# A column-group tail of three k tiles instead of four, with the last joined tile moved into the last column group's tail

## Chip, cores, metric

One core of one Trainium2 chip. The metric is device time of the whole kernel in microseconds, median of several executions. A profile is one execution, and its span is about 1.8 us shorter than the time of that execution.

## The reference

```python
B, S, D, W = 4, 4096, 4096, 64       # x [B,S,D], w [D,D] float32, offsets [B]
for b in range(B):
    o = int(offsets[b])
    results.append(x[b, o:o+W] @ w)  # 64 rows of each batch times the whole of w
```

So 256 rows are multiplied by a 4096 x 4096 matrix: 67 MB of w are read once, 4.2 MB are written. The rows are two stationary sets of 128 (`G = 2`); w has 32 k tiles of 128 rows.

## The kernel before

w is loaded by DMAs that cast to fp16 on the way. k tiles 1 to 27 come as blocks of whole rows, in buffers of four tiles, of which there are three. The last tiles (the tail) come as two column groups of 2048, so that the first group (`order[0]`) can be finished and stored while the last group (`order[1]`) still loads. The last two blocks of whole rows are the joined tiles: their products are not summed by themselves, but within the passes of the two column groups.

```python
blocks = [(0, 1), (1, 2), (3, 4), (7, 4), (11, 4), (15, 4), (19, 3), (22, 3), (25, 2), (27, 1)]
n_join = 2
k_tail = 28
...
order = [1, 0]
steps = [(ki, 2, 0, NG) for ki in range(k_tail, n_k, 2)]   # tail loads, per column group
...
join = range(blocks[-n_join][0], k_tail)                   # tiles 25, 26, 27
...
columns(order[1], list(join))               # last group: a first pass over the joined tiles
ng = order[0]
columns(ng, list(join) + list(range(k_tail, n_k)))         # first group: everything
for g in range(G):
    store(nc.gpsimd, g, ng * NG, (ng + 1) * NG)
ng = order[1]
k_fine = n_k - n_fine                       # the last two tiles, finer
for ki in range(k_tail, k_fine):            # last group: its tail
    for g in range(G):
        for j in range(n_sub):
            tail_mm(ki, g, ng, j, ki == k_tail, False)
q = [nc.scalar, nc.sync]
for g in range(G):
    for h in range(2):
        ...                                 # matmuls of tiles 30, 31, then one add
        add_out(4 * g + js[0], 2, g, ng * n_sub + js[0])
    store(q[g], g, ng * NG, (ng + 1) * NG)
```

`columns` runs the matmuls of one group, then adds half of the eight PSUM banks to the accumulator on VectorE, copies the other half out on ScalarE, and adds that too. The loads and the first group's stores are issued by GpSimd in one queue.

## Time and profile before

| | before |
|---|---|
| time, median | 181.62 us (181.52 to 181.75, 6 runs) |
| last load issued / landed | 134.12 / 169.14 us |
| first group's stores issued | 166.19 and 167.32 us |
| last store issued / landed | 174.88 / 179.0 us |

Here is the end of TensorE's timeline (start, duration, instruction, in brackets the idle time before it and what ended it):

```profile
149.24 14.42 PE L185 MATMUL banks<-wc,xT 128*128 128x512 f16 x64 [0.42 <-DMA wc<-in_w_dram]
164.29 3.63 PE L185 MATMUL banks<-wc,xT 128*128 128x512 f16 x16 [0.64 <-DMA wc<-in_w_dram]
169.18 3.61 PE L185 MATMUL banks<-wc,xT 128*128 128x512 f16 x16 [1.26 <-DMA wc<-in_w_dram]
```

TensorE finishes the first group at 163.66 and waits for loads three times: it has time to spare, 1.26 us of it ahead of the last stage. The first group's stores in GpSimd's timeline, and the last store's line among the DMA issues (KB, us from issue to landing):

```profile
166.19 0.55 POOL L231 DMA_DIRECT2D out_dram<-acc  x1 [31.34 <-DVE acc L244]
167.32 0.54 POOL L231 DMA_DIRECT2D out_dram<-acc  x1 [0.58 <-DVE acc L244]
...
out_dram<-acc SPq DMA_DIRECT2D x1, 1024.0 KB, 4.1
```

### The profile page before, as it was taken

Reading aid. Unit: us, or ns where it says so; the run is one execution under the profiler, and the core shown is the slowest. Engines: PE = TensorE matmul, PEld = TensorE weight load, DVE = VectorE, ACT = ScalarE, POOL = GpSimd, SP = SyncE. Lnnn points to the kernel's source line nnn. Section 1 sums busy time; section 2 is a strip of 40 time slices with the busy share of each in tenths; the row PEclk is TensorE's granted clock in tenths of the full one; section 3 lists DMA queues with packets and bytes.
Section 4 is the critical chain, followed back from the end, with each engine's and each line's share of the span. In section 5 each row is a group of like instructions: output and inputs, shape, how many; then the busy total and the mean of one; then the engine's idle time right before and its main releaser. Section 6 shows DMA issues by size and latency. Waiting matters only on the chain.

```text
span 179.9 us, 1393 instructions
## 1 busy us (share of the span) xinstructions
PE 123.0 (68%) x578; PEld 56.3 (31%) x578; DVE 83.2 (46%) x75; ACT 16.8 (9%) x15; POOL 11.1 (6%) x24
## 2 busy tenths in 40 slices
PE   1000007996399919990799649999939998998740
PEld 1000007642144404440344214444414443443310
DVE  2000004844046725662076605669956956308280
ACT  2402102644000000000000000000000004004000
POOL 4400000001000010001000100002060000000200
PEclk9999999999879999999699988999999999999997
DMA  6999997999999899999989999999999999999976
GB/s 200 315 261 215 226 262 168 219 237 233 226 226 211 189 197 233 237 219 226 219 189 197 233 220 208 217 224 202 235 200 219 191 211 216 212 215 214 363 337 288
DMA packets 3399, 40.97 MB, mean 228 GB/s; under 512 B 322, under 2 KB 322, under 8 KB 1346
## 3 DMA queue, kind: packets, MB, share of 16 engines
q0 software_dynamic: 2816, 36.70, 93.2%
q1 hardware_dynamic: 432, 3.15, 4.5%
q10 hardware_dynamic: 146, 1.05, 1.4%
q8 instruction: 4, 0.07, 0.1%
q14 instruction: 1, 0.01, 0.0%
HBM read 71.30 MB, written 4.19 MB: 420 GB/s over the span
## 4 chain that ended last, share of the span: by engine, by line
DMA 66%; PE 24%; POOL 2%; issue 2%; DVE 2%; DVEq 1%; POOLq 0%
DMA wc<-in_w_dram 66%; PE banks L185 24%; POOL wc L149 1%; DVE acc L195 1%; DVEq L292 1%; POOL xrow L131 1%; POOL wc L88 0%; DVE rows L122 0%; PE banks L119 0%; POOL below L100 0%; DVE rows L110 0%; POOL below L99 0%; DVE ones L115 0%; DVE off_f L116 0%; POOLq L100 0%
## 5 line engine op out<-in xcount | busy, mean ns | idle before, releaser
L185 PE MATMUL banks<-wc,xT 128*128 128x512 f16 x496 | 116.2, 390 | 22.5 <-DMA wc<-in_w_dram 22.4
L195 DVE TENSOR_TENSOR acc<-acc,banks 128x1024 f32<-128x1024 f32 x56 | 67.9, 1220 | 58.8 <-PE banks L185 57.6
L185 PEld LDWEIGHTS <-xT 128*128 128x128 f16 x512 | 50.7, 100 | 88.7 <-DMA wc<-in_w_dram 23.6
L171 PE MATMUL banks<-identity,xrow 128*128 128x128 f16 x64 | 5.2, 262 | 24.2 <-DMA xrow<-in_x_dram,rows 24.2
L180 DVE CAST xT<-banks 128x1024 f16<-128x1024 f32 x4 | 4.7, 1221 | 25.0 <-PE banks L171 25.0
L240 ACT COPY tmp<-banks 128x1024 f32<-128x1024 f32 x4 | 3.9, 1016 | 116.2 <-PE banks L185 116.2
L171 PEld LDWEIGHTS <-xrow 128*128 128x128 f16 x64 | 5.1, 127 | 24.3 <-DMA xrow<-in_x_dram,rows 24.3
L88 POOL DMA_DIRECT2D wc<-in_w_dram x9 | 5.0, 566 | 113.5 <-PE banks L185 112.7
L213 DVE COPY acc<-banks 128x1024 f32<-128x1024 f32 x4 | 4.9, 1225 | 4.6 <-PE banks L185 4.6
L185 PE MATMUL banks<-w,xT 128*128 128x512 f16 x16 | 6.1, 379 | 0.0
L182 ACT CAST xT<-banks 128x1024 f16<-128x1024 f32 x4 | 3.9, 1018 | 11.6 <-PE banks L171 11.6
L244 DVE TENSOR_TENSOR acc<-acc,tmp 128x1024 f32<-128x1024 f32 x4 | 4.7, 1218 | 0.0
L215 ACT COPY acc<-banks 128x1024 f32<-128x1024 f32 x4 | 4.0, 1012 | 6.5 <-PE banks L185 6.5
L149 POOL DMA_DIRECT2D wc<-in_w_dram x4 | 2.8, 721 | 9.3 <-PE banks L185 9.3
L231 POOL DMA_DIRECT2D out_dram<-acc x2 | 1.1, 549 | 31.9 <-DVE acc L244 31.9
L74 ACT CAST w<-acc 128x2048 f16<-128x2048 f32 x1 | 1.9, 1897 | 8.9 <-DMA acc<-in_w_dram 8.9
L119 PE MATMUL banks<-off_f,ones 1*128 1x4 f32 x2 | 0.6, 358 | 3.1 <-DVE off_f L116 3.1
L73 ACT CAST w<-acc 128x2048 f16<-128x2048 f32 x1 | 1.9, 1897 | 3.4 <-DMA acc<-in_w_dram 3.4
L110 DVE TENSOR_REDUCE rows<-below 128x1 f32<-128x128 f16 x1 | 0.3, 286 | 2.6 <-POOL below L100 2.6
L119 PEld LDWEIGHTS banks<-off_f,ones 1*128 1x128 f32 x2 | 0.5, 304 | 3.1 <-DVE off_f L116 3.1
L73 ACT ACT_TABLE_LOAD x1 | 1.3, 1283 | 1.3 <-PEq L281 1.3
L131 POOL DMA_INDIRECT xrow<-in_x_dram,rows x1 | 1.0, 1026 | 1.6 <-DVE rows L122 1.6
(11 smaller groups left out, 2.4 us busy)
## 6 DMA issues: line engine op xcount, KB each, us to landing
wc<-in_w_dram POOLq DMA_DIRECT2D x4, 4096.0 KB, 42.2
wc<-in_w_dram POOLq DMA_DIRECT2D x2, 3072.0 KB, 35.7
wc<-in_w_dram POOLq DMA_DIRECT2D x5, 1024.0 KB, 27.0
wc<-in_w_dram POOLq DMA_DIRECT2D x2, 2048.0 KB, 19.8
acc<-in_w_dram SPq DMA_DIRECT2D x2, 1024.0 KB, 10.5
out_dram<-acc POOLq DMA_DIRECT2D x2, 1024.0 KB, 6.1
out_dram<-acc ACTq DMA_DIRECT2D x1, 1024.0 KB, 3.9
out_dram<-acc SPq DMA_DIRECT2D x1, 1024.0 KB, 4.1
```

What stands on the lines that cost most here:

```text
L73: nc.scalar.copy(out=w_one[:, :NG], in_=w0_32[:, :NG])
L88: nc.gpsimd.dma_start(out=t[:, base : base + r * N], in_=w[k0 * P : (k0 + r) * P, :].rearrange("(p r) n -> p (r n)", r=r),)
L149: nc.gpsimd.dma_start(out=t[:, pos : pos + n * wd].rearrange("p (t n) -> p t n", t=n), in_=w[ki * P : (ki + n) * P, ng * NG + c0 : ng * NG ...
L171: nc.tensor.matmul(out=pairs[t][:, i * P : (i + 1) * P], lhsT=x_cols(g, 8 * t + i), rhs=identity[:], start=True, stop=True,)
L180: nc.vector.tensor_copy(out=dst, in_=pairs[t][:])
L182: nc.scalar.copy(out=dst, in_=pairs[t][:])
L185: nc.tensor.matmul(out=banks(bank), lhsT=xT[g][:, kt * P : (kt + 1) * P], rhs=rhs, start=start, stop=stop,)
L195: nc.vector.tensor_add(out=dst, in0=dst, in1=banks(bank, n))
L213: nc.vector.tensor_copy(out=dst, in_=banks(b0, 2))
L215: nc.scalar.copy(out=dst, in_=banks(b0, 2))
L240: nc.scalar.copy(out=tmp[g][:], in_=banks(4 * g + 2, 2))
L244: nc.vector.tensor_add(out=dst, in0=dst, in1=tmp[g][:])
```

## The change

Its intent: one k tile fewer in the half-row tail, one more in the row blocks (19 becomes a block of four), and less work in the last group's first pass, so that the first group's pass starts sooner.

```diff
-    blocks = [(0, 1), (1, 2), (3, 4), (7, 4), (11, 4), (15, 4), (19, 3), (22, 3), (25, 2), (27, 1)]
+    blocks = [(0, 1), (1, 2), (3, 4), (7, 4), (11, 4), (15, 4), (19, 4), (23, 3), (26, 2), (28, 1)]
     n_join = 2
-    k_tail = 28
+    k_tail = 29
...
-    steps = [(ki, 2, 0, NG) for ki in range(k_tail, n_k, 2)]
+    steps = [(k_tail, 1, 0, NG), (k_tail + 1, 2, 0, NG)]
...
-    columns(order[1], list(join))
+    columns(order[1], list(join)[:-1])
...
-    for ki in range(k_tail, k_fine):
+    for ki in range(k_tail - 1, k_fine):
...
-                tail_mm(ki, g, ng, j, ki == k_tail, False)
+                tail_mm(ki, g, ng, j, ki == k_tail - 1, False)
```

## The prediction

> **What bounds the kernel now.** I read the busy digits of the page first, then the chain, the issue-to-landing times of single loads, the TensorE timeline and one-microsecond windows of the last 20 us. The page:
>
> ```profile
> PE   1000007996399919990799649999939998998740
> DMA  6999997999999899999989999999999999999976
> DMA 66%; PE 24%; POOL 2%; issue 2%; DVE 2%; DVEq 1%; POOLq 0%
> wc<-in_w_dram POOLq DMA_DIRECT2D x4, 4096.0 KB, 42.2
> ```
>
> The 16 DMA engines are busy in almost every slice; TensorE has holes. The last line gives what lands per load: a block of 4 k tiles takes 42 us from issue to landing because another block is ahead of it in the queue. The chain of waits in order of time:
>
> ```profile
> 63.36 0.28 issue
> 63.65 41.99 DMA wc<-in_w_dram
> 105.64 0.05 issue
> 105.69 26.05 PE banks L185 x112
> 131.74 0.28 issue
> 132.02 2.10 POOL wc L149 x3
> 134.12 35.02 DMA wc<-in_w_dram
> 169.14 0.04 issue
> 169.18 1.04 PE banks L185 x4
> ```
>
> A load issued at 63.65 lands at 105.64, and the last tail load lands at 169.14. Adding each load's issue and its time to landing gives block (7,4) 67.0, (11,4) 86.3, (15,4) 105.64, (19,3) 120.1 (twice the median of 35.7 less 32.6, added to 81.28), (22,3) 134.6, (25,2) 144.4, (27,1) 149.2 and the four tail pieces 154.4, 159.3, 164.2, 169.14. So a k tile costs 4.84 us in the blocks of four, 4.82 in those of three, 4.8 to 4.9 in the small blocks, and 4.93 to 5.0 in the half-row tail pieces. 2.097 MB read in 4.84 us is 433 GB/s. **The load stream never starves and sets the time to 169 us.** What follows is the end, in windows (stretch; busy PE, PEld, DVE, ACT, POOL; clock; DMA share; GB/s moved):
>
> ```profile
> 166.00:167.00 1.00, 1.00 (x6) 0.49 (x5) 1.00 (x1) 0.00 (x0) 0.55 (x1) 1.00 1.09 221
> 167.00:168.00 1.00, 0.92 (x5) 0.29 (x3) 0.03 (x1) 0.00 (x0) 0.54 (x1) 1.00 1.01 311
> 168.00:169.00 1.00, 0.00 (x0) 0.00 (x0) 0.00 (x0) 0.00 (x0) 0.00 (x0) 1.00 1.00 401
> ...
> 172.00:173.00 1.00, 0.80 (x4) 0.18 (x2) 1.00 (x2) 0.00 (x0) 0.00 (x0) 1.00 0.47 197
> 173.00:174.00 1.00, 0.00 (x0) 0.00 (x0) 1.00 (x2) 0.00 (x0) 0.00 (x0) 1.00 0.68 287
> 174.00:175.00 1.00, 0.00 (x0) 0.00 (x0) 0.85 (x1) 0.00 (x0) 0.00 (x0) 1.00 0.95 401
> ```
>
> Loads count fp16 bytes written (about 217 GB/s); stores count fp32 bytes (400 and more). So the bytes of the loads end near 167.4, though the last one's completion arrives at 169.14, and the stores of the first finished column group run from 167.4 on. The DMA engines then have about 0.85 us of idle (0.53 + 0.32) in 172 to 174, waiting for the last group's stores, issued at 172.63 and 174.88 and landed 3.9 and 4.1 us later.
>
> **What the Trainium skill says.** (1) "DMA: Bandwidth & Descriptors", section "Where 436 GB/s comes from": the ceiling is 435.2 GB/s from the SBUF ports. The trace agrees: 433 read. A faster load stream is not to be had by reordering. (2) Same page, "Issuing engines are not separate DMA queues": transfers from different issuers interleave on the same 16 engines. The trace agrees: three issuers' stores together never move more than 467 GB/s in a microsecond. (3) Same page, "Anatomy of one DMA": a fit for the GpSimd path of 2.0 us plus bytes over 436 GB/s. For 1.05 MB that is 4.4 us; the trace has 3.9 and 4.1 from the other two issuers, so a last store cannot be shortened here. (4) "TensorE: Matmul & The Clock Gate", Part 1: 215.7 ns per warm 512-column matmul, 426.7 ns cold. The trace agrees: outputs of eight matmuls follow each other by 1.725 us (216 ns each); after the wait that ends at 105.69 the first eight take 3.24 us (405 ns) at a granted clock of 0.58.
>
> **The change, part by part.**
> Unchanged: 512 matmuls of the product, 56 adds of 1220 ns out of PSUM (six blocks with 8 adds before and after, plus the column groups), number of loads, bytes of loads and stores.
>
> *Load stream.* One k tile leaves the half-row tail for a row block, saving 4.95 - 4.84 = 0.1 us. Landings after: (19,4) 105.64 + 4 x 4.84 = 125.0; (23,3) + 14.5 = 139.5; (26,2) + 9.8 = 149.3; (28,1) + 4.8 = 154.1; first group's tail 29 at 156.6 and 30-31 at 161.5; last group's 29 at 164.0 and 30-31 at 169.0.
>
> *Issue of the tail loads.* They reuse the buffer of block 19, so they wait for 4 k tiles rather than 3. TensorE ends (15,4) at 121.4 as before, then idles 3.6 us until 125.0 (before it went straight on, as 120.1 lay behind it), then runs 64 matmuls. That took 15.7 us after idles of 4.06 and 4.02 us and 14.2 us after 3.6 us (67.0 to 81.2). So block 19 ends at 139.2 to 140.7 instead of 131.7, and the tail is issued by 144. The queue has work until 154.1: 10 us of margin, **no starvation**.
>
> *TensorE behind the stream.* Block (23,3) with the two-tile first pass of the last group is 64 matmuls, for which 14.16 us were measured on the same mix: 153.5 to 154.9. The first group's pass then has 24 matmuls (26-28) at 216 ns = 5.2, plus the 0.6 us by which the same stage now exceeds 64 x 216 ns (14.42 against 13.8; banks still being emptied): 159.3 to 160.7. Tile 29 adds 8, 1.7 us: 161.0 to 162.4. Tiles 30-31 (landed 161.5) add 16, 3.45 us. **The first group ends at 165.0 to 165.9, against 163.65 before: 1.3 to 2.2 us later**, because less of it can be done ahead: its last piece lands at 161.5 rather than 159.3.
>
> *Last group before the last landing.* Tiles 28-29 are 16 matmuls as before (3.63 us with the bank wait, some 3.75 here): done at 168.8 to 169.65, against 167.9 before. Before, TensorE waited 1.26 us for the last load; now the last stage begins at 169.0 to 169.65 instead of 169.18: -0.15 to +0.5. The stage itself (16 matmuls, four adds, two stores) is the same.
>
> *Stores of the first group.* They were issued 2.53 and 3.66 us after its last matmul (166.19, 167.32), hence now at 167.5 to 168.4 and 168.7 to 169.6. Before, bytes ran about 1.2 us after issue, just when the loads' bytes ended. Now the store bytes begin at 168.7 to 169.6, so the engines are idle for 1.4 to 2.3 us that they used before. Four stores of 1.05 MB at 435 GB/s need 9.64 us: bytes end at 178.3 to 179.2. Before: 167.4 + 9.64 + 0.85 idle = 177.9 (the windows show about 178.2), landed at 179.0. With the same 0.8 us of completion: 179.1 to 180.0. **Sum: +0.1 to +1.0 us, middle near +0.5**; the 0.1 us saved on loads is in it.
>
> **Rivals.**
> *A: nothing is seen.* If the late stores only fill the 0.85 us hole and the last group starts at 169.0, the end is the last landing plus the same 10 us: 181.6. For it: the hole is there, and TensorE had 1.26 us to spare. Against: the stores shift by more than the hole.
> *B: a real gain.* If the shorter tail lets the half-row transfers go (each k tile 0.1 us dearer), or an idle of TensorE was on the path, 181.0 or so. For it: the tail loads are the dearest bytes. Against: only one of 32 k tiles changes, and the rate is at 433 GB/s already.
> *C: TensorE becomes the bound.* Another cold start at 125.0 and again in the tail would push the first group's end to 167 and the last stage to 171: 183.5. For it: the wait before 125.0 is new, 3.6 us, about the length after which the clock was seen low. Against: from 139.5 on TensorE has hardly any wait, and (7,4) after 3.6 us was not slowed much.
> *D: the load queue runs dry* since the tail is issued 7 to 9 us later. For it: the longer reuse chain. Against: 10 us of margin.
>
> **Range and chances.** Before is 181.72 (181.58 to 181.75). My sum gives +0.5 with a spread of +0.1 to +1.0, rival A pulls down, C up: 182.1. I take 181.3 (A with a part of B) to 183.1 (half of C) as 8 in 10. Over 2% would be under 178.1 or over 185.4; the first needs a load stream above the measured rate, the second needs D or a double C. So 0.02, 0.95, 0.03.
>
> **What would show it.** Right: last load landing within 0.3 us of 169.0; TensorE idle before (19,4) of about 3.6 us and the tail issued near 140; first group's stores issued at 167.5 or later; no hole in the DMA share in 172 to 174 but one near 168; last store issued at 174.7 to 175.4 and landing 4 to 5 us later. Wrong: a last landing clearly before 168.8 (loads cheaper than I think) or after 169.6 (dry queue or slower tail); first group's stores as early as before; a cold clock in the tail.

## The result

| | before | after |
|---|---|---|
| time, median of 6 | 181.62 us (181.52 to 181.75) | 182.63 us (182.37 to 183.77) |
| last load landed | 169.14 | 169.1 |
| first group's stores issued | 166.19, 167.32 | 168.13, 169.28 |
| last store issued, landing | 174.88, 4.1 us | 175.05, 4.7 us |

The ratio of after to before is 1.0068, 95% interval 1.0039 to 1.0096: slower, by well under 2%. A ratio is the mean time of one kernel's fast runs over that of the other's in the same rounds, so it is not quite the ratio of the medians. The spread of these six is larger too, 1.4 us against 0.2; but twelve later runs of the kernel before, beside e1 to e4 below, spread by 1.4 us as well (181.57 to 182.99).

The page of the changed kernel, its busy digits and the shares of the chain:

```profile
PE   1000008998499919993899859982999999999920
DMA  6999998999999989999999999998999999999696
DMA 47%; PE 40%; issue 3%; DVE 3%; another core or an unknown queue 2%; POOL 1%; DVEq 1%; POOLq 0%
```

TensorE's share of the chain went from 24% to 40%, and DMA's digits have a 6 in the third slice from the end, where they had a 9. In the chain in order of time one sees where TensorE took over:

```profile
82.96 42.13 DMA wc<-in_w_dram
125.09 0.05 issue
125.14 27.33 PE banks L185 x118
...
155.95 8.38 PE banks L185 x38
...
166.76 3.63 PE banks L185 x16
```

The chain meets no load after 125.09, the landing of block 19. The TensorE and GpSimd timelines say the same:

```profile
125.14 47.82 PE L185 MATMUL banks<-wc,xT 128*128 128x512 f16 x208 [3.96 <-DMA wc<-in_w_dram]
...
168.13 0.57 POOL L231 DMA_DIRECT2D out_dram<-acc  x1 [24.52 <-DVE acc L244]
169.28 0.53 POOL L231 DMA_DIRECT2D out_dram<-acc  x1 [0.57 <-DVE acc L244]
...
out_dram<-acc SPq DMA_DIRECT2D x1, 1024.0 KB, 4.7
```

After a new wait of 3.96 us, 208 matmuls run in one stretch; none waits for a load again. The first group's stores are issued 1.94 and 1.96 us later. The last store lands 0.8 us later than before: its issue came 0.17 us later, and it takes 0.6 us longer to land. The windows of one microsecond (busy PE, PEld, DVE, ACT, POOL; clock; DMA share; GB/s) show what that does to the DMA engines:

```profile
167.00:168.00 1.00, 1.00 (x6) 0.46 (x5) 1.00 (x2) 0.00 (x0) 0.00 (x0) 1.00 0.52 102
168.00:169.00 1.00, 1.00 (x6) 0.48 (x5) 0.97 (x1) 0.00 (x0) 0.57 (x1) 1.00 0.11 20
169.00:170.00 1.00, 1.00 (x7) 0.41 (x6) 0.00 (x0) 0.00 (x0) 0.53 (x1) 1.00 0.89 377
...
173.00:174.00 1.00, 0.00 (x0) 0.00 (x0) 1.00 (x2) 0.00 (x0) 0.00 (x0) 1.00 1.05 442
```

Where 311 and 401 GB/s were moved before, the engines are now idle for 1.37 us (0.48 + 0.89). The hole that the kernel before had in 172 to 174 is gone: once begun, all four stores run without a pause. In windows of a quarter of a microsecond nothing is moved from 168.5 to 169.25, and the last bytes come at 179.0: 4.19 MB in 9.75 us, or 430 GB/s.

### The profile page after: what moved, and what is told of

Same layout as the page of the kernel before. It is cut to its first block, busy times and chain, and to the rows that moved or that the text cites.

```text
span 180.6 us, 1393 instructions
## 1 busy us (share of the span) xinstructions
PE 128.0 (71%) x578; PEld 58.6 (32%) x578; DVE 83.4 (46%) x75; ACT 17.0 (9%) x15; POOL 10.8 (6%) x24
## 3 DMA queue, kind: packets, MB, share of 16 engines
q10 hardware_dynamic: 146, 1.05, 1.4%
HBM read 71.30 MB, written 4.19 MB: 418 GB/s over the span
## 4 chain that ended last, share of the span: by engine, by line
DMA 47%; PE 40%; issue 3%; DVE 3%; another core or an unknown queue 2%; POOL 1%; DVEq 1%; POOLq 0%
DMA wc<-in_w_dram 47%; PE banks L185 40%; DVE acc L195 2%; DVEq L292 1%; POOL xrow L131 1%; POOL wc L88 0%; DVE rows L122 0%; PE banks L119 0%; POOL below L100 0%; DVE rows L110 0%; POOL below L99 0%; DVE ones L115 0%; DVE off_f L116 0%; POOLq L100 0%
## 5 line engine op out<-in xcount | busy, mean ns | idle before, releaser
L185 PE MATMUL banks<-wc,xT 128*128 128x512 f16 x496 | 120.1, 400 | 17.7 <-DMA wc<-in_w_dram 17.4
L185 PEld LDWEIGHTS <-xT 128*128 128x128 f16 x512 | 51.8, 102 | 86.6 <-DMA wc<-in_w_dram 19.9
L171 PE MATMUL banks<-identity,xrow 128*128 128x128 f16 x64 | 6.5, 299 | 24.1 <-DMA xrow<-in_x_dram,rows 24.1
L171 PEld LDWEIGHTS <-xrow 128*128 128x128 f16 x64 | 6.3, 143 | 24.2 <-DMA xrow<-in_x_dram,rows 24.2
```

The lines of the kernel that those rows point to most:

```text
L171: nc.tensor.matmul(out=pairs[t][:, i * P : (i + 1) * P], lhsT=x_cols(g, 8 * t + i), rhs=identity[:], start=True, stop=True,)
L185: nc.tensor.matmul(out=banks(bank), lhsT=xT[g][:, kt * P : (kt + 1) * P], rhs=rhs, start=start, stop=stop,)
```

## The experiments

Theory T after the result. T1: the late stores of the first group leave the DMA engines idle, and the last store then queues behind them. T2: the clock, low after the new wait, delays TensorE. Rivals: only the start of the last matmul stage counts (R); the block shapes or the smaller tail loads cost time; the first group's stores are hidden anyway. Each run's before is the kernel before on the same chip, in the same rounds; runs of different series are compared by their ratios. There is no e8 on record.

| run | median, us | before, us | ratio (95%) |
|---|---|---|---|
| e1, tail of three alone | 184.03 | 181.72 | 1.0124 (1.011 to 1.0139) |
| e2, moved tile alone | 181.67 | 181.72 | 0.9999 (0.9986 to 1.0012) |
| e3, after, early stores | 182.38 | 181.72 | 1.0036 (1.0023 to 1.0048) |
| e4, after, clock kept up | 182.17 | 181.72 | 1.0028 (1.0015 to 1.0041) |
| e5, before, late stores | 183.25 | 181.63 | 1.0077 (1.0058 to 1.0095) |
| e6, before, half stores | 181.81 | 181.63 | 1.0015 (0.9991 to 1.0039) |
| e7, after, half stores | 182.34 | 181.63 | 1.0048 (1.002 to 1.0077) |
| e9, after, e3 and e4 | 182.07 | 181.63 | 1.0021 (1.0003 to 1.0038) |
| e10, as e9, 15 fillers | 181.92 | 181.76 | 1.0011 (0.9998 to 1.0024) |
| e11, after again | 182.37 | 181.76 | 1.0031 (1.0018 to 1.0044) |
| e12, before, early stores | 181.96 | 181.76 | 1.0007 (0.9993 to 1.0021) |

### The two parts alone

The tail of three without the second part (against the changed kernel):

```diff
-    columns(order[1], list(join)[:-1])
+    columns(order[1], list(join))
-    for ki in range(k_tail - 1, k_fine):
+    for ki in range(k_tail, k_fine):
-                tail_mm(ki, g, ng, j, ki == k_tail - 1, False)
+                tail_mm(ki, g, ng, j, ki == k_tail, False)
```

> The new blocks and the tail of three, but tile 28 stays in the last group's first pass. Theory T (the first group's stores come late, the DMA engines idle before them, and the four stores then run back to back to the end): 8 more matmuls lie ahead of the first group's end, 1.7 us; its stores are issued near 169.9 and 171.0 instead of 168.1 and 169.3, the hole in the DMA share grows by 1.7 us and the time goes from 182.6 to about 184.3. Rival R (only the start of the last matmul stage counts): that stage has 8 matmuls fewer ahead of it in exchange, starts near 169.4 as in the changed kernel, and the time stays at 182.6.

Measured: 184.03. The stores were issued at 169.91 and 171.06, the last stage's first add began at 170.67, only 0.26 us later than in the changed kernel. Windows of this run, and its last store's line:

```profile
168.00:169.00 1.00, 0.89 (x5) 0.32 (x4) 1.00 (x2) 0.49 (x1) 0.00 (x0) 1.00 0.15 29
169.00:170.00 1.00, 1.00 (x6) 0.45 (x5) 1.00 (x2) 0.00 (x0) 0.09 (x1) 1.00 0.00 0
170.00:171.00 1.00, 1.00 (x6) 0.48 (x5) 1.00 (x2) 0.00 (x0) 0.49 (x1) 1.00 0.00 0
...
out_dram<-acc SPq DMA_DIRECT2D x1, 1024.0 KB, 6.2
```

Two whole microseconds pass in which nothing is moved, and the last store lands 6.2 us after its issue, against 4.7. That is T1, and R alone is out: the last stage hardly moved, the time rose by 1.4 (ratios 1.0124 and 1.0068). The second part of the change is thus a repair of the first: it takes 8 matmuls from ahead of the first group's end.

The moved tile alone, on the kernel before (join 25 to 27, tail of four):

```diff
-    columns(order[1], list(join))
+    columns(order[1], list(join)[:-1])
-    for ki in range(k_tail, k_fine):
+    for ki in range(k_tail - 1, k_fine):
-                tail_mm(ki, g, ng, j, ki == k_tail, False)
+                tail_mm(ki, g, ng, j, ki == k_tail - 1, False)
```

> The old blocks and the tail of four, with the last joined tile (27) moved into the last group's tail. T: the first group ends sooner (about 163, set by the landing at 159.3 plus 16 matmuls), its stores are issued by 165.6, but queue behind loads whose bytes end at 167.4: no gain, 181.6 (181.4 to 181.8). The last load is still waited for by TensorE for some 0.7 us. Rival: if a longer tail of the last group costs by itself, 182.2 or more.

Measured: 181.67, the same as before. The stores were issued at 165.21 and 166.34, 1 us sooner than before, and began no sooner: they lie in the queue behind the loads. So the whole loss comes with the tail of three.

### Late stores on the kernel before

```diff
+    nc.gpsimd.tensor_copy(
+        out=x16.bitcast(fp32)[:, :NG], in_=acc[0][:, ng * NG : (ng + 1) * NG]
+    )
     for g in range(G):
         store(nc.gpsimd, g, ng * NG, (ng + 1) * NG)
```

> Kernel before with a GpSimd copy of 2048 columns ahead of the first group's stores, which delays them by d (some 2 us, to be read from the trace) and touches no matmul. T1: up to about 1.2 us the delay fits the idle of the DMA engines between 172 and 174; beyond that every microsecond counts: 181.7 + (d - 1.2), so 182.5 for d = 2, 183.5 for d = 3, with the last store issued at 174.9 as before and landing later. Rival (the first group's stores are hidden anyway): 181.7.

The copy took 2.81 us and the stores were issued from 169.12 on, 2.9 us later than 166.19. The formula gives 181.7 + 2.9 - 1.2 = 183.4; measured 183.25, against 181.63 of its before. GpSimd's timeline, TensorE's last stage and the last store:

```profile
169.12 1.09 POOL L231 DMA_DIRECT2D out_dram<-acc  x2
...
169.22 3.61 PE L185 MATMUL banks<-wc,xT 128*128 128x512 f16 x16 [1.25 <-DMA wc<-in_w_dram]
...
out_dram<-acc SPq DMA_DIRECT2D x1, 1024.0 KB, 5.7
```

The last matmul stage starts as before, with 1.25 us to spare, and the last store was issued at 174.92; it only lands later, 5.7 us after its issue. Late stores of the first group cost time by themselves, with blocks, tail and TensorE unchanged. The rival "hidden anyway" is out.

The traces give T1 as one number. From the issue of the first group's first store to the landing of the last store it is 11.6 us in the changed kernel (168.13 to 179.75), 11.6 in e1 (169.91 to 181.51) and 11.5 here (169.12 to 180.62), and 11.6 to 11.7 in e4, e7 and e11 below: each microsecond of delay is paid in full. In the kernel before it is 12.8 us (166.19 to 178.98), so its stores had 1.2 us to spare. There the end hangs on the last store alone, which lands 4.0 to 4.2 us after its issue in every trace in which the first group's stores were not late (before, e2, e3, e9, e10, e12).

### Clock kept up

12 matmuls whose result is never used, run in the wait before block 19 of the changed kernel:

```diff
     for k0, r in blocks[2:-n_join]:
+        if k0 == 19:
+            for _ in range(12):
+                nc.tensor.matmul(out=banks(0), lhsT=xT[0][:, :P],
+                                 rhs=xT[0][:, :NT], start=True, stop=True)
         whole_rows(range(k0, k0 + r))
```

> Changed kernel with 12 matmuls of no use in the wait before block 19, so that its 64 matmuls start at full clock. T: block 19 ends 1.9 us sooner, but block 23 lands at 139.6 and the first group's last piece at 161.7, so that group ends near 165.2 (0.4 sooner) and the time falls by about 0.4 to 182.2; the spread between runs (182.4 to 183.8) shrinks to some 0.3, as the slow start no longer reaches the end. R (the slow clock is the whole cause): 181.7.

Measured: 182.17, with a spread of 0.3 (182.07 to 182.36), both as T2 said. Block 19's 64 matmuls took 13.97 us, and the last store was issued at 174.80 instead of 175.05. The changed kernel was then run again for a second trace:

> The changed kernel again, for a second trace of it beside these runs: 182.4 to 183.8 by the earlier runs, median 182.6. T2: between 125 and the end its matmuls take another time than the 47.82 us of the first trace if the clock came up sooner or later, and the last store moves with it; the last load lands within 0.2 us of 169.1 all the same.

Median 182.37 (182.11 to 182.50). Against its own before this is 1.0031, and the run with the fillers is 1.0028: the medians do not show that the fillers gain anything, and the spread is only 0.4 without them. TensorE's timeline of this second trace of the same kernel, and its last store:

```profile
124.93 13.99 PE L185 MATMUL banks<-wc,xT 128*128 128x512 f16 x64 [3.61 <-DMA wc<-in_w_dram]
139.43 21.52 PE L185 MATMUL banks<-wc,xT 128*128 128x512 f16 x96 [0.51 <-DMA wc<-in_w_dram]
161.76 10.97 PE L185 MATMUL banks<-wc,xT 128*128 128x512 f16 x48 [0.81 <-DMA wc<-in_w_dram]
...
174.81 0.35 SPq L231 DMA_DIRECT2D out_dram<-acc  x1
...
out_dram<-acc SPq DMA_DIRECT2D x1, 1024.0 KB, 4.7
```

The last store is issued a little before that of the kernel before (174.88), and still lands 0.5 us later: with TensorE undisturbed T1 alone remains.

Here the clock was up by itself after a wait of 3.61 us: block 19 took 13.99 us and was done before block 23 had landed, as in the run with the fillers (182.17 profiled there, 182.19 here). In the first trace the first add after block 19's landing came 3.06 us after the start of its matmuls, against 1.94 us here, and the next 2.29 us later, against 1.73 us; (3.06 - 1.94) + (2.29 - 1.73) = 1.7 us were lost to the low clock. So the changed kernel has two kinds of execution. Of the 1.7 us, 0.24 us reach the last store's issue (175.05 against 174.81). That the slow start makes the spread between runs is not shown (see what stays open, below). In both kinds the first group's stores are late (167.90 and 169.04 even here), since the group's last piece now lands at 161.7 instead of 159.3.

### Early stores, and both remedies

The first group's stores are issued right behind the tail loads with stale data. Its output is wrong, which doesn't matter for the time.

```diff
-    for g in range(G):
-        store(nc.gpsimd, g, ng * NG, (ng + 1) * NG)      # after the first group
...
+    first = order[0]
+    stale = x16.bitcast(fp32)
+    for g in range(G):
+        nc.gpsimd.dma_start(
+            out=out_rows[g, :, first * NG : (first + 1) * NG],
+            in_=stale[:, g * NG : (g + 1) * NG])
     columns(order[1], list(join)[:-1])
```

> Changed kernel, but the first group's stores send stale data (a wrong result on purpose) and are issued right after the tail loads, so they queue straight behind them; TensorE's work is untouched. T: the hole at 167.5 to 169.1 goes, the last store is issued at 175.0 as before the edit of this run and lands in about 4.1 us instead of 4.7: 182.0, 0.6 less than the changed kernel. R (TensorE's lateness) or load shapes: no gain, 182.6.

Measured: 182.38, less of a gain than expected; by the ratios (1.0036, and 1.0031 for the changed kernel again) none. In its trace the last store landed after 4.0 us, not 4.7, so T1's part came out; but TensorE needed 48.83 us for the 208 matmuls instead of 47.82, and issued the last store at 175.90: the granted clock was 0.50 from 125 to 130:

```profile
124.99 48.83 PE L185 MATMUL banks<-wc,xT 128*128 128x512 f16 x208 [3.61 <-DMA wc<-in_w_dram]
...
125.00:128.00 3.00, 3.00 (x8) 1.07 (x9) 0.00 (x0) 0.00 (x0) 0.00 (x0) 0.50 1.11 238
```

In that execution the slow start ate the gain. Its wait, 3.61 us, is the same as in e11, where the clock was up, and in e1 the clock was low after only 2.60 us: in these traces the length of the wait does not tell which start comes. Hence both remedies at once:

> Changed kernel with both remedies: the 12 matmuls that keep the clock up before block 19, and the first group's stores sent early with stale data (a wrong result on purpose). Theory T, now in two parts (T1: the late first-group stores lengthen the last store from 4.1 to 4.7 us; T2: the slow clock after the new wait delays the last matmul stage by 0.2 to 1 us, differently from run to run): last store issued at 174.8, landing 4.0 us later, 181.5, as the kernel before, with a spread under 0.4. If something else in the change costs time (block shapes, the tail's smaller pieces), it stays at 181.9 or more.

The profiled execution was as expected: 181.58, last store issued at 174.85 and landed 4.1 us later. But the median was 182.07, with 182.46 as the highest: a miss by 0.5, and a spread of 0.9 where under 0.4 was expected. Two runs looked for the remainder. The control, early stores in the kernel before:

> Control for the early store: the kernel before, with the first group's stores sent early with stale data (a wrong result on purpose). T1: in the kernel before these stores already begin when the loads' bytes end, so nothing moves: 181.7, last store landing about 4.1 us after its issue. If the early store itself costs time, 182.0 or more, and the 0.4 us that was left over with both remedies is its cost.

Measured 181.96 against 181.76, with the profiled execution at 182.30. Its TensorE line of the last stage:

```profile
169.72 3.61 PE L185 MATMUL banks<-wc,xT 128*128 128x512 f16 x16 [1.72 <-DMA wc<-in_w_dram]
```

The last load's completion came at 169.7 here, though the change from the loads' rate to the stores' took place in 167 to 168 as in the kernel before (283 GB/s in that microsecond, 311 there). To take out small shifts of the whole stream, count from the landing of the first group's last piece to that of the last load. With a tail of four this is 9.8 us in the kernel before, e2, e5 and e6, and 10.3 in e12; with a tail of three it is 7.4 us in the changed kernel, e1, e4, e7 and e11, and 7.6, 7.8 and 7.8 in e3, e9 and e10. So in all four traces with early stores the completion of the load ahead of them came 0.2 to 0.5 us later, and the remedy is not free; why is not shown.

> As the run with both remedies, with 15 matmuls of no use instead of 12, so that the wait before block 19 is nearly filled (3.4 of 3.6 us; a wrong result on purpose again). If the 0.4 us that was left over came from a clock that still dropped in some runs, 181.6 with a spread under 0.4; if from the small margin of TensorE before the last load (0.27 us against 1.26 before) or elsewhere, 182.0 as with 12.

Measured 181.92, spread 0.3. This is the control's 181.96: on one chip and in the same rounds, the changed kernel gave 182.37, with both remedies 181.92, and the kernel before with the same early stores 181.96. With both causes taken away nothing of the change is left to explain, within the noise: the ratios to the kernel before are 1.0011 and 1.0007, each to about 0.0013, so the two differ by 0.1 us, give or take some 0.35. Block shapes and smaller tail loads are bounded by that and no more closely.

### Half stores

The last group's stores are cut in four, each sent after its own add, alternating between ScalarE's and SyncE's queue:

```diff
             add_out(4 * g + js[0], 2, g, ng * n_sub + js[0])
-        store(q[g], g, ng * NG, (ng + 1) * NG)
+            c0 = (ng * n_sub + js[0]) * NT
+            store(q[h], g, c0, c0 + 2 * NT)
```

> Kernel before with the last group's stores cut in four halves, each sent after its own add. T1: the idle of the DMA engines in 172 to 174 is filled and the last store is half as long: bytes end at 167.4 + 9.64 = 177.1 instead of 178.2, time about 180.6. Rival (the last add and a fixed store time set the end): a half store saves 1.2 us, 180.5. The same here; it is the pair with the next run that tells them apart.

> Changed kernel with the last group's stores cut the same way. T1: the DMA engines are busy without a hole from 169.1 to 179.0, so cutting and sending earlier moves nothing: 182.3 to 182.6. Rival (the last add and a fixed store time set the end): 1.2 us less, 181.4.

On the kernel before: 181.81, a miss of 1.2 us. On the changed kernel: 182.34, as expected. The windows of the first and its last store's line:

```profile
173.00:174.00 1.00, 0.00 (x0) 0.00 (x0) 1.00 (x2) 0.00 (x0) 0.00 (x0) 1.00 0.93 381
...
177.00:178.00 1.00, 0.00 (x0) 0.00 (x0) 0.00 (x0) 0.00 (x0) 0.00 (x0) 0.66 0.75 307
```

The hole is filled, as meant, but the last half store still landed 4.1 us after its issue near 174.8, so at 178.9 instead of 179.0. Adding the DMA shares from 167 to 179, the engines were busy for 10.75 us against 10.58 in the kernel before, and in the last microseconds not all of them had work left (0.75, then 0.10). So the hole in 172 to 174 was not worth its 0.85 us: 0.1 us lay in it by the trace, and nothing by the median (181.81 against 181.63). T1's number for this run was wrong, because in the kernel before the end hangs on the last store's issue and landing, not on the bytes of all four stores; and half the bytes did not land sooner. The rival that both kernels gain 1.2 us is out as well. No version beats the kernel before, and none was suggested by the runs: in it the stores begin when the load bytes end, and filling the idle time that is left gained nothing.

## Why the prediction was right, point by point

- **Load stream.** Right. Block 19 landed at 125.09 (125.0 predicted), the last load at 169.1 (169.0). The 0.1 us from the smaller tail cannot be seen: 169.1 against 169.14, and from trace to trace it comes anywhere between 168.8 and 169.2. One reading was not exact: that the loads' bytes end near 167.4. In the changed kernel, where no store covers it, a last part of them runs on, at 115 GB/s and less, until 168.5.
- **Issue of the tail loads.** Right. TensorE idled for 3.96 us (3.6); block 19 was done near 140.8 in one trace and at 138.9 in the other (139.2 to 140.7, so just outside at either end), and no load came late. Rival D is out.
- **First group.** Right, 165.6 (165.0 to 165.9), worked out as the start of its first add, 164.35, plus the 1.26 us by which that add started before the last matmul in the kernel before.
- **Last stage.** Right: it begins 1.06 us before its first add, at 169.35 (169.0 to 169.65).
- **First group's stores.** Right: issued at 168.13 and 169.28, in the stated windows. The hole near 168 and the closed hole near 173 are there. e1 and e5 show that this causes the loss.
- **Bytes end, sum.** Right, term by term. With the measured issue of the first store put in, the sum gives 168.13 + 1.2 + 9.64 + 0.8 = 179.77; the last store landed at 179.75. In the second trace it gives 179.54, and the landing was at 179.51. These are 0.8 and 0.5 us later than before, where +0.1 to +1.0 with a middle of +0.5 was said. The part of the sum that was left wide is when the first group ends, and with it the first store's issue; the low clock moved that from 167.90 to 168.13. I had it as an upper edge of the block's time and as rival C.
- **The medians.** They rose by 1.0 us in the first six runs and by 0.6 in the later five. The first figure is at the very edge of the sum, and more than its own trace shows: two slow executions that were not traced push it up. That it stayed within the sum is in part luck.
- **Rates.** That three issuers' stores never move more than 467 GB/s in a microsecond held only in the trace that was read: e5 shows 492 and 508. Such a short window does not show a ceiling.
- **Rival C** holds in part: TensorE had no wait for a load after 125.14 in the first trace. It was not a second cold start, though, and the end moved mostly through the stores.
- **Rivals A and B** fell: the shift of the stores (1.94 us) was larger than the hole (0.85), and nothing was gained; what the tail's size is worth is known only to the bound above.

What stays open: the slowest executions (183.31 and 183.77 of the changed kernel, 182.97 and 183.81 with half stores, 182.99 of the kernel before) were timed, not traced, so their cause is not known. The mean granted clock of each run, as a mean over the whole kernel, settles nothing about one block, but it speaks against the low clock for the two slowest: 183.77 and 183.81 have 0.954, as has the trace of e11 with its full clock, while the fastest of the first six, 182.37, has 0.921.

## What to carry to other kernels

When a load stream keeps the DMA engines busy to its end, shortening what follows it depends on having the next transfer ready at the moment the stream's bytes end; here an early output that came 2 us late left the DMA engines idle though the last matmuls were in time. Two sums decided the end, whichever was later: the first output's issue plus 11.6 us for all four stores, or the last output's issue plus some 4.1 us. Count the room between the last landing of the early part and that of the late part: here a tail of four tiles gives the first group 169.14 - 159.3 = 9.8 us to be finished in, a tail of three 169.1 - 161.7 = 7.4 us. A new wait of TensorE (2.6 to 4.0 us here) ahead of a stretch without slack can also start that stretch at a low clock, in some executions and not in others.

## What the Trainium skill lacked or had wrong

- "DMA: Bandwidth & Descriptors", "Where 436 GB/s comes from", says that for transfers between HBM and SBUF an HBM limit of about 358 GB/s binds. With one core at work the load stream here read 433 GB/s, near the 435 GB/s that the same section gives for the ports (and it notes a measurement of 425 itself). So the sentence does not hold for one core at work.
- Same page, "Anatomy of one DMA": the fit of 2.0 us plus bytes over 436 GB/s is for one GpSimd transfer and does not say what a store from another engine takes behind others. Here the last store, of 1.05 MB, took 4.0 to 4.2 us where the first group's stores were not late, and 4.7, 5.7 and 6.2 us behind late ones; one of half that size, behind three other halves, still took 4.1 us.
- Same page, on the completion of a transfer: it gives no figure for what stores queued behind a load do to the completion of that load. With such stores the last load completed 0.2 to 0.5 us later, counted from the landing of the first group's last piece, in four traces of four; the nine others agree with each other to 0.1 us.
- "TensorE: Matmul & The Clock Gate", Part 1, calls the window free-running and the start variable, and the traces agree: after the same wait of 3.61 us block 19 began at a granted clock of 0.50 in one trace (e3) and at full clock in another (e11). What it lacks is a case like this one, in which the stretch that follows has no slack: the low clock lengthened the block by 1.7 us and put off the last store's issue by 0.24 us.
